# Near scores of the second prompt half: 32 consecutive queries against 160 keys, rows put in class order by DMA

## The chip, the core and the metric

The kernel runs on one core of one Trainium2 chip. The metric is device time in microseconds (us) of one execution; lower is better. The core has TensorE (PE, with its weight loads PEld), VectorE (DVE), ScalarE (ACT), GpSimd (POOL) and SyncE (SP), which only issues DMAs here. SBUF has 128 partitions; matmuls accumulate in PSUM.

## The reference, cut to what matters

One layer of a decoder for a prompt of 256 tokens and 32 sample tokens, all in f32. One input projection gives, among others, q, k and v for three groups of four heads of dimension 128. Group g attends to keys at distances that are multiples of its dilation (1, 4, 16):

```
GROUPS = ((128, 1), (512, 4), (2048, 16))          # window, dilation
valid = (du >= 0) & (du <= BAND) & (uk >= 0)       # BAND = 128 steps of the dilation
sc = q . k * ATT_SCALE - slope * distance, -inf where not valid
p = softmax(sc); o = p @ v
# head j of the three groups is merged with weights softmax(lse) over the groups
```

So a token of group 0 (dilation 1, "near") can see itself and the 128 tokens before it: 129 keys. Merging three groups by their log-sum-exp equals one softmax over the keys of all three groups, and the kernel computes it so. Around the attention stand a gated convolution, two large projections, two layer norms and a feed-forward part of width 5632.

## The kernel before, in words

All activations lie with features on partitions and the 288 tokens on the free axis. Nearly all time goes into `product` (L237): one block of 128 output features, 16 blocks of 128 inputs, three matmuls each (high and low part of the weights and of x in a 32-bit replicated form), so 48 matmuls of 288 columns. The weights of a block come as a 1 MB DMA into `wst` (three buffers, `prepare`, L194), then ACT casts the high part (`whi`) and DVE subtracts it to get the low part (`wlo`), in two halves (`split`, L263). There are four half buffers, so the split of a block starts when PE is done with a half of the block two before it.

The order of the work on each engine is settled when the program is built: the framework simulates a timeline and places each instruction by priority of program order and by when it expects it to be ready. `behind(i, after)` adds an order edge without a wait. `prepare`, called in `product`, traces a block's load and split ahead of the matmuls of the block before; after each `product`, `prompt_step` (L228) pops some queued small copies (`soon`) and runs the next step of the current prompt generator, up to its next `yield`.

The prompt attention works in four classes c: token t belongs to class t mod 4 (NC = 4, NW = 32 tokens per class and half). For groups 1 and 2 a query needs keys of its own class only. So queries, scores and weights of a half h (128 tokens) are stored in class order: partition c*32+i holds token 4*i+c. The scores of a half are one row of SBUF, `s_half[h]`: first the near columns (128 for h = 0, 256 for h = 1), then the far columns of groups 1 and 2.

`score_row(heads)` (L471) issues the score matmuls on PE in a fixed row: for each head, half, group and class one matmul with 32 stationary columns (the queries of that class) that writes 32 partitions of PSUM (L490). For the near group all four quadrants take the same keys: the first 128 for h = 0, all 256 for h = 1, though a query of the second half can see only 129 of them; the rest is masked by large distances in `m_near[1]`. If weights of earlier heads are waiting (`o_next`), `output_row` (L430, matmuls at L443) follows at once in the same row.

`softmax(j, s3)` (L506) adds the distance penalties on DVE (L512), one instruction per half and group, from PSUM into `s_half`; then for each half reduce_max (L519), scaling by -SCALE (L520), exp with a sum on ACT (L521), reciprocal and scaling (L522, L523). `weights(p)` then transposes all scores in blocks of 32 (L455, one DVE instruction) into `s_squares`, and `moved` copies the blocks to their places: the diagonal ones on POOL (L459), the others on ACT (L463) or DVE (L461) from the queue `soon`. `no_keys` (L504) is a memset on POOL that masks the far columns without keys in the first half.

`three_heads` (heads 2, 0, 1 in this order; two steps each) and `last_head` (head 3) are the generators that run these; `last_head` begins with the score row that also holds the outputs of the first three. Beside them `sample_steps` runs the sample's attention on POOL, ACT and DVE over 1 MB cache tiles. `load_distances(h)` (L396) brings the distances into SBUF, rows in class order: `m_near[h]` and, through `m_all[h]`, `m_far` (L406). At L843 the queries are copied from PSUM into `q_all` in class order (L846).

Of the kernel before, what the change touches and what calls it, by code (L numbers as in the profile page):

```python
# [12 lines left out]
AF = mybir.ActivationFunctionType  # L13
ALU = mybir.AluOpType
AX = mybir.AxisListType
PSUM = bass.MemoryType.PSUM

P = 128
D = 2048
KD = D // P  # L20
SEQ = 256
# [13 lines left out]
NG, NH = 3, 4  # L35
DIL = (1, 4, 16)
BAND = 128
SCALE = P**-0.5
# [4 lines left out]
BIG = 1e30  # L43
# [4 lines left out]
NC = 4  # L48
NI = SEQ // NC
NW = P // NC  # L50

NQ = P // 32
N_NEW = NT + NG - 1
MB = 1 + 2 + 2
SLOPE = [[float(np.float32(2.0 ** (-8.0 * (g * NH + j + 1) / (NG * NH)))) for j in range(NH)] for g in range(NG)]
# [52 lines left out]
def layer_kernel(ctx: ExitStack, tc: tile.TileContext, ins, outs):  # L108
# [14 lines left out]
    def sb(pl, shape, tag, dt=F32, bufs=None):  # L123
        return pl.tile(shape, dt, tag=tag, name=nm(tag), bufs=bufs)
# [22 lines left out]
    w_load = [None]  # L147
# [3 lines left out]
    def behind(i, after):  # L151

        tc.add_manual_dep(i.ins, after.ins.name, no_sync, reason="pace")
# [202 lines left out]
    def pa_take(n):  # L356
        pa_at[0] += n
        return pa[:, pa_at[0] - n : pa_at[0]]


    m_near = [pa_take((1 + h) * P) for h in range(2)]
    m_all = [pa_take((NG - 1) * (1 + h) * P).rearrange("p (g k) -> p g k", g=NG - 1) for h in range(2)]
    k_third = [m_all[1].rearrange("p g k -> p (g k)")[:, g * SEQ : (g + 1) * SEQ] for g in range(NG - 1)]
    k_first = pa_take(SEQ)
    m_far = pa_take(2 * (NG - 1) * NI).rearrange("p (h g k) -> p h g k", h=2, g=NG - 1)

# [29 lines left out]
    def load_distances(h):  # L396

        c0, nk = (C_M0, C_M1)[h], (1 + h) * P
        m = ins["cst"][:, c0 : c0 + NG * nk].rearrange("(i c) (g k) -> c i g k", c=NC, g=NG)
        for c in range(NC):  # L400
            at = slice(c * NW, (c + 1) * NW)
            behind(sp.dma_start(m_near[h][at], m[c, :, 0]), w_load[0])
            behind(sp.dma_start(m_all[h][at], m[c, :, 1:]), w_load[0])
        for c in range(NC):
            at = slice(c * NW, (c + 1) * NW)
            pool.tensor_copy(  # L406
                m_far[at, h, :, : (1 + h) * NW], m_all[h][at].rearrange("p g (i c) -> p c g i", c=NC)[:, c]
            )

    def in_a_row(row):  # L410

# [13 lines left out]
    def far_keys(h, g):  # L425

        at = (1 + h) * P + (g - 1) * NI
        return slice(at, at + (1 + h) * NW)
# [42 lines left out]
    def score_row(heads):  # L471

        s3 = []
        w = P + (NG - 1) * NW
        first = att()
        row = [last_mm[0]]
        for n, (j, kT, k_class) in enumerate(heads):
            second = sb(ps, [P, 512], *(("att", F32, 2), ("long", F32, 1), ("acc",))[n])
            near_at = second[:, 3 * P :] if n == 2 else first[:, n * w : n * w + P]
            far_at = first[:, n * w : (n + 1) * w - P] if n == 2 else first[:, n * w + P : (n + 1) * w]  # L480
            s3.append([
                [near_at, *(far_at[:, g * NW : (g + 1) * NW] for g in range(NG - 1))],
                [second[:, far_keys(1, g) if g else slice(0, 2 * P)] for g in range(NG)],
            ])
            for h in range(2):
                for g in range(NG):
                    for c in range(NC):
                        at = slice(c * NW, (c + 1) * NW)
                        k = k_class[g - 1][:, c, : (1 + h) * NW] if g else kT[:, : (1 + h) * P]
                        row.append(pe.matmul(  # L490
                            s3[n][h][g][at], q_all[:, j, g, h * P + c * NW : h * P + (c + 1) * NW], k,
                            start=True, stop=True,
                        ))
        if o_next:
            some_moves(len(soon))
            row += output_row()
        in_a_row(row)
        return s3
# [4 lines left out]
    def no_keys():  # L503
        pool.memset(s_half[0][:, P:].rearrange("p (g k) -> p g k", g=NG - 1)[:, :, NW:], -BIG)  # L504

    def softmax(j, s3):  # L506
        s = s_half
        for h in range(2):
            near = (1 + h) * P
            for g in range(NG):  # L510
                at = far_keys(h, g) if g else slice(0, near)
                dve.scalar_tensor_tensor(  # L512
                    s[h][:, at], m_far[:, h, g - 1, : (1 + h) * NW] if g else m_near[h], -SLOPE[g][j] / SCALE,
                    s3[h][g],
                    ALU.mult, ALU.add,
                )
        for h in range(2):
            st = sb(wk, [P, 4], "st", bufs=4)
            dve.reduce_max(st[:, 0:1], s[h], AX.X)  # L519
            dve.tensor_scalar_mul(st[:, 1:2], st[:, 0:1], -SCALE)  # L520
            act.activation(s[h], s[h], AF.Exp, bias=st[:, 1:2], scale=SCALE, accum_out=st[:, 2:3])  # L521
            dve.reciprocal(st[:, 3:4], st[:, 2:3])  # L522
            dve.tensor_scalar_mul(s[h], s[h], st[:, 3:4])  # L523

    def values(vT):
        squares(v_squares[:, :2], vT[:, 0, :SEQ].rearrange("p (b k) -> p b k", b=2))
# [6 lines left out]
    def weights(p):  # L533

        some_moves(len(soon))
        squares(s_squares, s_all)
        moved(p, s_squares)
# [6 lines left out]
    def three_heads(heads, vT):  # L544

        no_keys()
        s3 = score_row(heads)
        pause[0] = N_PAUSE
        n_moves[0] = N_MOVES_TWO
        for n, j in enumerate((2, 0, 1)):  # L550
            softmax(j, s3[j])
            yield 1
            weights(p_three[j])
            no_keys()
            if n == 0:
                values(vT)
                moved(v_three[2], v_squares, True)
            yield 1
        o_next.extend(zip(range(3), v_three, p_three))

    def last_head(head, vT):

        s3 = score_row([head])
        softmax(head[0], s3[0])
        values(vT)
        moved(late_v, v_squares)
        yield 1
        weights(late_p)
        yield 2
        o_next.append((head[0], late_v, late_p))  # L570
# [272 lines left out]
    for j in range(NH):  # L843
        for g in range(NG):
            q = (q_first.pop(0) if q_first else product(x)).rearrange("p h a -> p (a h)")
            act.copy(  # L846
                q_all[:, j, g].rearrange("p (h c i) -> p h c i", h=2, c=NC),
                q[:, :SEQ].rearrange("p (h i c) -> p h c i", h=2, c=NC),
            )
            act.copy(q_s[:, g, j], q[:, SEQ:])  # L850
            n = j * NG + g
            if n in (5, 7):
                load_distances((n - 5) // 2)
            elif n in (3, 6):
                behind(sp.dma_start(*((cst, ins["cst"][:, :C_BM]) if n == 3 else (prm, ins["prm"]))), w_load[0])
            steps_on[0] = j * NG + g >= NH * NG - 1 - LATER
# [612 lines left out]
```

## Time and profile before

| | |
|---|---|
| median of 3 runs | 1701.44 us (1701.07 to 1701.99) |
| profiled execution | 1701.29 us, of which the span of the trace is 1699.5 us |
| granted clock | 0.999 |
| busy: PE, DVE, ACT, POOL | 100%, 70%, 55%, 23% of the span |
| HBM | 307 GB/s over the span |
| score rows of the prompt | from 182.34 us (heads 0 to 2) and from 220.96 us (head 3 and the outputs of the first three) |

Rows of the profile read: engine, line of the kernel, operation, output and inputs by the program's tile names, shape, count; then busy us and mean ns, and the idle time just before with what ended it. Timeline rows begin with the start in us and the time that the merged row covers. Tile names are those of the memory pools, so several things share one: `yal` holds scores, distances, `by_time` and the high parts of transposed values; `yah` holds queries and weights; `dd` keys and values. SPq and ACTq are the instruction streams that issue DMAs.

### The profile page before, as it was taken

To read this page: it belongs to the slowest core of one execution; us is meant where nothing else is said; L and a number is where in the kernel's file an instruction comes from. 1 tells how busy PE (TensorE), PEld (TensorE's weight loads), DVE (VectorE), ACT (ScalarE), POOL (GpSimd) and SP (SyncE) were. 2 spreads that over 40 slices of the span, in tenths; PEclk is the share of its full clock that TensorE was granted. 3 is DMA by queue.
4 is the path that set the end of the run, shared out by engine and by line. 5 is a ranking of instruction groups with operands and counts; after the bars stand their busy time and mean duration, and the time that the engine had idled before them with its cause. 6 is when DMAs were issued, how large, how long until landed. Compare 5 with 4: busy or idle time off the path is not lost.

```text
span 1699.5 us, 34306 instructions
## 1 busy us (share of the span) xinstructions
PE 1693.1 (100%) x14094; PEld 1689.8 (99%) x14094; DVE 1197.2 (70%) x1549; ACT 941.7 (55%) x1683; POOL 396.7 (23%) x528
## 2 busy tenths in 40 slices
PE   9999999999999999999999999999999999999998
PEld 9999999999999999999999999999999999999998
DVE  5476779889887777655888886776554555555576
ACT  6477686665666655544546664555433454444455
POOL 0122242223332121111454440111100010011175
PEclk9999999999999999999999999999999999999999
DMA  8788778666688889577766668676666666766553
GB/s 316 271 298 351 282 284 314 241 251 245 248 295 311 333 305 337 212 262 255 282 234 225 224 214 322 224 257 226 229 238 225 223 227 248 294 223 250 197 176 113
DMA packets 61532, 436.16 MB, mean 257 GB/s; under 512 B 7936, under 2 KB 11904, under 8 KB 23680
## 3 DMA queue, kind: packets, MB, share of 16 engines
q1 hardware_dynamic: 60080, 430.15, 69.0%
q10 hardware_dynamic: 1296, 3.83, 0.6%
q8 instruction: 110, 1.80, 0.4%
q14 instruction: 46, 0.38, 0.1%
HBM read 427.50 MB, written 94.53 MB: 307 GB/s over the span
## 4 chain that ended last, share of the span: by engine, by line
PE 99%; DMA 0%; DVE 0%; ACT 0%; SPq 0%; issue 0%; ACTq 0%; DVEq 0%
PE acc L257 32%; PE acc L258 32%; PE acc L259 32%; PE acc L342 1%; PE acc L443 0%; DMA yah<-in_x 0%; PE att L490 0%; DVE acc L1140 0%; PE acc L490 0%; SPq L297 0%; DVE yah L1140 0%; ACT xh L309 0%; PE acc L1129 0%; PE acc L1126 0%; PE acc L1125 0%
## 5 line engine op out<-in xcount | busy, mean ns | idle before, releaser
L263 DVE TENSOR_TENSOR wlo<-wst,whi 128x1024 fp32r<-128x1024 f32 (+1 forms) x579 | 744.9, 1288 | 394.0 <-ACT whi L263 391.7
L263 ACT CAST whi<-wst 128x1024 fp32r<-128x1024 f32 (+1 forms) x579 | 588.6, 1019 | 653.8 <-PE acc L258 587.2
L257 PE MATMUL acc<-xh,whi 128*128 128x288 f32 (+1 forms) x3216 | 920.3, 286 | 0.0
L258 PE MATMUL acc<-xl,whi 128*128 128x288 f32 (+1 forms) x3216 | 920.0, 286 | 0.0
L259 PE MATMUL acc<-xh,wlo 128*128 128x288 f32 (+1 forms) x3216 | 920.0, 286 | 0.0
L257 PEld LDWEIGHTS acc<-xh,whi 128*128 128x128 f32 x3216 | 607.8, 189 | 0.5 <-issue 0.4
L258 PEld LDWEIGHTS acc<-xl,whi 128*128 128x128 f32 x3216 | 607.8, 189 | 0.0
L259 PEld LDWEIGHTS acc<-xh,wlo 128*128 128x128 f32 x3216 | 607.8, 189 | 0.0
L258 PE MATMUL acc<-yal,whi 128*128 128x288 f32 x1216 | 347.5, 286 | 0.0
L259 PE MATMUL acc<-yah,wlo 128*128 128x288 f32 x1216 | 347.4, 286 | 0.0
L257 PE MATMUL acc<-yah,whi 128*128 128x288 f32 x1216 | 347.2, 286 | 0.0
L258 PEld LDWEIGHTS acc<-yal,whi 128*128 128x128 f32 x1216 | 229.8, 189 | 0.0
L259 PEld LDWEIGHTS acc<-yah,wlo 128*128 128x128 f32 x1216 | 229.7, 189 | 0.0
L257 PEld LDWEIGHTS acc<-yah,whi 128*128 128x128 f32 x1216 | 229.6, 189 | 0.0
L909 POOL COPY qk_s<-u 128x2 f32<-128x2 f32 x44 | 37.3, 847 | 534.5 <-ACT u L1228 487.0
L897 DVE SCALAR_TENSOR_TENSOR cy<-u,prm,cy 128x304 f32<-128x304 f32 x120 | 70.5, 587 | 7.0 <-ACT cy L895 4.4
L613 POOL TENSOR_TENSOR cache<-cache,cst 128x1024 f32<-128x1024 f32 x16 | 32.8, 2056 | 112.2 <-DMA cache<-in_cv 105.0
L613 POOL TENSOR_TENSOR cache<-cache,qk_s 128x1024 f32<-128x1024 f32 x16 | 32.7, 2045 | 65.6 <-DMA cache<-in_ck 65.3
L920 DVE TENSOR_TENSOR ya<-cy,acc 128x256 f32<-128x256 f32 x104 | 27.6, 308 | 26.7 <-PE acc L259 26.2
L263 ACT CAST yah<-ya 128x288 fp32r<-128x288 f32 x76 | 32.6, 428 | 23.6 <-DVE ya L920 14.6
L611 ACT ACTIVATE cache<-cache,qk_s 128x128 f32<-128x128 f32 x128 | 40.6, 392 | 0.0
L611 ACT ACTIVATE cache<-cache,cst 128x128 f32<-128x128 f32 x128 | 40.0, 389 | 0.0
(282 smaller groups left out, 1186.6 us busy)
## 6 DMA issues: line engine op xcount, KB each, us to landing
wst<-in_w_in SPq DMA_DIRECT2D x112, 1024.0 KB, 5.5
wst<-in_w_up SPq DMA_DIRECT2D x88, 1024.0 KB, 4.9
cache<-in_ck SPq DMA_DIRECT2D x18, 1024.0 KB, 8.3
cache<-in_cv SPq DMA_DIRECT2D x18, 1024.0 KB, 8.5
wst<-in_w_a SPq DMA_DIRECT2D x16, 1024.0 KB, 6.7
wst<-in_w_out SPq DMA_DIRECT2D x16, 1024.0 KB, 4.9
wst<-in_w_down SPq DMA_DIRECT2D x32, 512.0 KB, 4.6
wst<-in_w_down SPq DMA_DIRECT2D x16, 1024.0 KB, 4.9
```

What stands on the lines that cost most here:

```text
L257: pe.matmul(out, hi[:, c, :], xh_k, start=k == 0, stop=False)
L258: pe.matmul(out, hi[:, c, :], xl_k, start=False, stop=False)
L259: last_mm[0] = pe.matmul(out, lo[:, c, :], xh_k, start=False, stop=k == nk - 1)
L263: return act.copy(hi, src), dve.tensor_tensor(lo, src, f32(hi), ALU.subtract)
L342: i = pe.matmul(o[b], first_w(term == 2, b, k), xk, start=k == 0 and term == 0, stop=k == KD - 1 and term == 2,)
L611: behind(act.activation(o[:, a, b], t[:, a, b], AF.Copy, scale=w[:, a, b : b + 1]), w_split[0])
L613: behind(pool.tensor_tensor(o, t, w.unsqueeze(3).broadcast_to([P, *n]), ALU.mult), w_split[1])
L897: dve.scalar_tensor_tensor(y, u[:, i : i + YW], prm[:, w0 + i : w0 + i + 1], y, ALU.mult, ALU.add)
L909: pool.tensor_copy(dst[:, 0:2], u[:, SEQ : SEQ + 2])
L920: dve.tensor_tensor(a, b, c, ALU.mult)
```

## The change

The near scores of the second half are computed for 32 queries in succession in time, t = 32*c to 32*c+31, instead of 32 queries of one class. These need only the 160 keys from 32*c to 32*c+159 (of 256), so each quadrant gets its own window of keys: NB_W = 160. Groups 1 and 2 and the first half stay in class order. The near scores of the second half then come out in time order: DVE adds the penalties per quadrant into the new buffer `by_time` (128 x 256, filled with -BIG once; it lies where the distances `m_all[0]` lay), and four DMAs of SP copy rows c, c+4, c+8, ... of it to quadrant c of `s_half[1]`, after which the softmax goes on as before. `softmax` is divided into `scored` (penalties) and `softmax(h)` (one half), and the order of the steps changes: the penalties of the next head are written in the step of the head before, the DMAs are issued once that head's weights have left `s_half`, and the second half's softmax of the first head comes one step later. The queries of the near group are stored in class order for the first half and in time order for the second, with two copies. The distances `m_near[1]` are loaded as windows of 160.

```diff
+NB_W = P + 32
...
-    m_near = [pa_take((1 + h) * P) for h in range(2)]
+    m_near = [pa_take(n) for n in (P, NB_W)]
+    pa_take(2 * P - NB_W)
...
+    by_time = m_all[0].rearrange("p g k -> p (g k)")
...
-            behind(sp.dma_start(m_near[h][at], m[c, :, 0]), w_load[0])
+            if h:
+                n = c0 + c * NW
+                behind(sp.dma_start(m_near[h][at], ins["cst"][at, n : n + NB_W]), w_load[0])
+            else:
+                behind(sp.dma_start(m_near[h][at], m[c, :, 0]), w_load[0])
...
+        if h:
+            pool.memset(by_time, -BIG)
...
-                [second[:, far_keys(1, g) if g else slice(0, 2 * P)] for g in range(NG)],
+                [second[:, far_keys(1, g) if g else slice(0, NB_W)] for g in range(NG)],
...
-                        k = k_class[g - 1][:, c, : (1 + h) * NW] if g else kT[:, : (1 + h) * P]
+                        if g:
+                            k = k_class[g - 1][:, c, : (1 + h) * NW]
+                        else:
+                            k = kT[:, c * NW : c * NW + NB_W] if h else kT[:, :P]
...
-    def softmax(j, s3):
+    def later_near(j, s3):
+
+        for c in range(NC):
+            at = slice(c * NW, (c + 1) * NW)
+            dve.scalar_tensor_tensor(
+                by_time[at, c * NW : c * NW + NB_W], m_near[1][at], -SLOPE[0][j] / SCALE, s3[1][0][at],
+                ALU.mult, ALU.add,
+            )
+
+    def by_class_rows():
+
+        for c in range(NC):
+            at = slice(c * NW, (c + 1) * NW)
+            behind(sp.dma_start(s_half[1][at, : 2 * P], by_time[c::NC]), w_load[0])
+
+    def scored(j, s3):
         s = s_half
         for h in range(2):
-            near = (1 + h) * P
-            for g in range(NG):
-                at = far_keys(h, g) if g else slice(0, near)
+            for g in range(h, NG):
+                at = far_keys(h, g) if g else slice(0, P)
                 dve.scalar_tensor_tensor(
...
-        for h in range(2):
-            st = sb(wk, [P, 4], "st", bufs=4)
...
+    def softmax(h):
+        s = s_half
+        st = sb(wk, [P, 4], "st", bufs=4)
+        dve.reduce_max(st[:, 0:1], s[h], AX.X)
...
-        for n, j in enumerate((2, 0, 1)):
-            softmax(j, s3[j])
+        order = 2, 0, 1
+        later_near(order[0], s3[order[0]])
+        by_class_rows()
+        for n, j in enumerate(order):
+            scored(j, s3[j])
+            softmax(0)
+            if n:
+                softmax(1)
+            if n < 2:
+                later_near(order[n + 1], s3[order[n + 1]])
             yield 1
+            if n == 0:
+                softmax(1)
             weights(p_three[j])
             no_keys()
+            if n < 2:
+                by_class_rows()
...
     def last_head(head, vT):
 
         s3 = score_row([head])
-        softmax(head[0], s3[0])
+        later_near(head[0], s3[0])
+        by_class_rows()
+        scored(head[0], s3[0])
+        softmax(0)
         values(vT)
         moved(late_v, v_squares)
         yield 1
+        softmax(1)
         weights(late_p)
...
+            n = SEQ if g else P
             act.copy(
-                q_all[:, j, g].rearrange("p (h c i) -> p h c i", h=2, c=NC),
-                q[:, :SEQ].rearrange("p (h i c) -> p h c i", h=2, c=NC),
+                q_all[:, j, g, :n].rearrange("p (h c i) -> p h c i", h=n // P, c=NC),
+                q[:, :n].rearrange("p (h i c) -> p h c i", h=n // P, c=NC),
             )
+            if n < SEQ:
+                act.copy(q_all[:, j, g, n:], q[:, n:SEQ])
```

More of the change, by code (lines that the diff above doesn't have):

```diff
@@ L516, in softmax @@
                 )
-        for h in range(2):
-            st = sb(wk, [P, 4], "st", bufs=4)
[L519 to L523, printed above, removed]
+    def softmax(h):
+        s = s_half
+        st = sb(wk, [P, 4], "st", bufs=4)
+        dve.reduce_max(st[:, 0:1], s[h], AX.X)
+        dve.tensor_scalar_mul(st[:, 1:2], st[:, 0:1], -SCALE)
+        act.activation(s[h], s[h], AF.Exp, bias=st[:, 1:2], scale=SCALE, accum_out=st[:, 2:3])
+        dve.reciprocal(st[:, 3:4], st[:, 2:3])
+        dve.tensor_scalar_mul(s[h], s[h], st[:, 3:4])
     def values(vT):
```

## The prediction

> **What bounds the kernel now.** I read the page first: engines, clock, and the chain that ended last.
>
> ```profile
> span 1699.5 us, 34306 instructions
> PE 1693.1 (100%) x14094; PEld 1689.8 (99%) x14094; DVE 1197.2 (70%) x1549; ACT 941.7 (55%) x1683; POOL 396.7 (23%) x528
> PE 99%; DMA 0%; DVE 0%; ACT 0%; SPq 0%; issue 0%; ACTq 0%; DVEq 0%
> ```
>
> TensorE is busy for 1693.1 of 1699.5 us and it is 99% of the chain (the windows below show its granted clock at 1.00). Then the waits of PE alone, over the whole span:
>
> ```profile
> PE acc L273 <- PEq L1456: 0.8, 1, 0.8
> PE acc L342 <- ACT yal L309: 0.4, 1, 0.4
> ```
>
> These are all its waits, both at the very start. So nothing that another engine does now ends late for PE. Only two things can move the time: PE has less or more to stream, or something becomes so late that PE begins to wait. The change does a little of the first and works on the second.
>
> **PE: what goes.** The timeline of PE over the score rows of the first three heads (start, duration, then the instruction; each group of four quadrants counts 8 because an f32 matmul is recorded as two):
>
> ```profile
> 182.34 0.43 PE L490 MATMUL att<-yal,yah 128*32 128x128 f32 x8
> 182.58 0.31 PE L490 MATMUL att<-u,yah 128*32 128x32 f32 x16
> 182.71 0.62 PE L490 MATMUL att<-yal,yah 128*32 128x256 f32 x8
> 183.14 0.41 PE L490 MATMUL att<-u,yah 128*32 128x64 f32 x16
> 183.36 0.40 PE L490 MATMUL att<-dd,yah 128*32 128x128 f32 x8
> ```
>
> Starts give the throughput. The near group with 256 keys takes 183.14 - 182.71 = 0.43 us, the one with 128 keys 182.58 - 182.34 = 0.24 us. The slope is 0.19 us per 128 keys; 96 keys fewer are worth 0.14 us, or 0.16 us if the whole 0.43 scales with length (0.43 x 96/256). Four heads: 0.57 to 0.64 us. I take 0.6 us. PE has no idle time there, so all of it shortens the span: 0.035%, the entire possible gain on PE.
>
> Each quadrant now gets its own 160 keys instead of one shared stream. Could the four quadrants then run one after the other? The far groups already give each quadrant its own keys, and two groups of 64 keys fit in 0.22 us, which is 0.11 us per group, a quarter of the 0.43 us that 256 keys take. So they overlap. If they did not, four streams of 0.27 us (0.43 x 160/256) would replace 0.43 us: +0.65 us a head, +2.6 us in all.
>
> **Early edits.** Loading the distances has as many DMAs as before (the near one has rows of 160 instead of 256 values), plus one memset of 256 columns on POOL. The query of the near group is copied in two ACT instructions instead of one, four times in the span. The rows around one such copy:
>
> ```profile
> 48.03 0.37 ACT L846 COPY yah<-acc 128x256 f32<-128x256 f32 x1
> 50.02 1.05 ACT L263 CAST whi<-wst 128x1024 fp32r<-128x1024 f32 x1 [1.54 <-PE acc L258]
> ```
>
> ACT sits idle for 1.54 us right behind the copy, waiting for PE. Two copies cost at most twice 0.37 us, so 0.37 us more, inside 1.54 us: nothing. The memset: POOL is 23% busy over the span and nothing on PE waits for it: nothing. Without this cover each copy would delay a cast, four times 0.37 us.
>
> **DVE: what is added.** The score additions, grouped by shape:
>
> ```profile
> L512 DVE SCALAR_TENSOR_TENSOR yal<-yal,att 128x128 f32<-128x128 f32 x3 | 0.8, 278 | 0.0
> L512 DVE SCALAR_TENSOR_TENSOR yal<-yal,att 128x256 f32<-128x256 f32 x2 | 0.8, 409 | 0.0
> L512 DVE SCALAR_TENSOR_TENSOR yal<-yal,att 128x64 f32<-128x64 f32 x4 | 0.7, 211 | 0.0
> ```
>
> One addition of 256 columns (0.41 us) becomes four of 160 columns on 32 partitions. No row has that shape; time goes with columns, so 0.28 us is the lower and 0.41 us the upper bound, 0.31 us by interpolation. Four are 1.24 us (1.12 to 1.64), so +0.83 us a head (+0.71 to +1.23). The stage of the first three heads, from the windows view (busy of PE, PEld, DVE, ACT, POOL, then clock, DMA share, GB/s):
>
> ```profile
> 185.50:197.20 11.70, 11.70 (x99) 11.70 (x96) 8.84 (x30) 7.64 (x18) 4.73 (x9) 1.00 0.59 225
> 197.20:208.90 11.70, 11.70 (x98) 11.70 (x97) 11.04 (x29) 9.66 (x23) 3.38 (x5) 1.00 0.59 216
> 208.90:221.00 12.10, 12.10 (x103) 11.96 (x105) 8.84 (x15) 10.46 (x27) 6.15 (x9) 1.00 0.64 233
> ```
>
> DVE is busy 8.84 + 11.04 + 8.84 = 28.7 of 35.5 us: 6.8 us free, of which 2.5 us are taken. It fits on average, tightest in the middle.
>
> **The new waits.** Each head puts 4 DMAs of 32 KB on SP's queue, from by_time to s_half. Three engines can be held by them. DVE: in the first step it writes the next head's near scores into by_time, after the DMAs have read it; behind that stands the rest (wlo) of a weight split. DVE again: reduce_max of the second half waits for the DMAs to land. SP: the DMAs wait for DVE, and weight loads queue behind them. First SP's loads, the rows being a load, its landing time, and the cast that reads that block three loads later:
>
> ```profile
> 184.65 9.57 SPq L205 DMA_DIRECT2D wst<-in_w_in  x2
> ```
> ```profile
> wst<-in_w_in SPq DMA_DIRECT2D x1, 1024.0 KB, 8.0
> ```
> ```profile
> 200.56 1.05 ACT L263 CAST whi<-wst 128x1024 fp32r<-128x1024 f32 x1
> ```
>
> The load issued at 184.65 lands at 192.65; its cast starts at 200.56. A load may be 7.9 us later at no cost, while the DMAs hold SP only until DVE has written, and then for four issues. Cost: nothing; past 7.9 us SP's delay would reach the cast one for one. Now DVE and the steps that set PE's deadlines:
>
> ```profile
> 185.48 0.39 PE L257 MATMUL acc<-xh,whi 128*128 128x288 f32 x1
> 186.01 0.23 DVE L512 SCALAR_TENSOR_TENSOR yal<-yal,att 128x32 f32<-128x32 f32 x2
> 189.80 0.85 DVE L455 STREAM_TRANSPOSE yah<-yal 128x640 f32<-128x640 f32 x1
> 190.56 1.18 DVE L263 TENSOR_TENSOR wlo<-wst,whi 128x1024 fp32r<-128x1024 f32 x1
> 203.61 0.84 DVE L455 STREAM_TRANSPOSE yah<-yal 128x640 f32<-128x640 f32 x1
> 212.74 0.84 DVE L455 STREAM_TRANSPOSE yah<-yal 128x640 f32<-128x640 f32 x1 [0.20 <-ACT yah L463]
> 220.96 0.42 PE L490 MATMUL att<-dd,yah 128*32 128x128 f32 x8
> ```
>
> From 185.48 to 220.96 PE runs six products, 5.91 us each. The wlo at 190.56 belongs to the third, which starts at 185.48 + 2 x 5.91 = 197.3. It ends at 191.74 now, so DVE has 5.6 us to give.
>
> How long do the DMAs take? The nearest rows are other DMAs of 16 to 64 KB, loaded early between weight loads: 32 KB ones, then the issue times in ns and the spread of landing of one line's.
>
> ```profile
> yal<-in_cst SPq DMA_DIRECT2D x8, 32.0 KB, 5.5
> ```
> ```profile
> L403 SPq DMA_DIRECT2D yal<-in_cst x8: 311/417/443, 25.6 to 40.9; - x8
> ...
> DMA to landing us min/median/max: 1.8/5.5/7.6
> ```
>
> So an issue takes 0.42 us, and L, from issue to landing, lies between 1.8 and 7.6 us. For the first head I take 5.3 us: near scores ready at 186.0 + 1.24 = 187.2, last issue 3 x 0.42 = 1.3 us later, and the load of 184.65 lands at 192.65, with the class rows behind it. For the other two the DMA share is about 0.6: 0.6 x 5.5 + 0.4 x 1.8 = 4.0 us, my choice. The first wait on DVE then ends at 187.2 + 1.3 + 5.3 = 193.8; adding 1.24 us and wlo's 1.18 us, wlo ends at 196.2 even if it is queued behind: 1.1 us before its deadline. Hidden, but not by much; past L = 6.4 us it would cost PE one for one, at this place.
>
> The weights' chain is the second deadline. Where PE reads them (moves of the second head's weights on ACT, then the output row on PE):
>
> ```profile
> 216.18 0.66 ACT L463 COPY yah<-yah 32x160 f32<-32x160 f32 x2
> 217.56 2.00 ACT L463 COPY yah<-yah 32x160 f32<-32x160 f32 x6
> 219.57 1.32 ACT L463 COPY yah<-yah 32x160 f32<-32x160 f32 x4
> 221.98 2.38 PE L443 MATMUL acc<-yah,yal 128*32 128x256 f32 x96
> 224.17 1.28 PE L443 MATMUL acc<-yah 128*32 128x256 f32 x48
> 225.38 0.39 PE L257 MATMUL acc<-xh,whi 128*128 128x288 f32 x1
> ```
>
> The last head in order is the second of three in the row, so PE needs it about a third into 221.98 to 225.38: 223.1. Its 12 moves take 3.98 us, so the transpose ahead of them (212.74 to 213.58 now) must end by 219.1. The chain after the change, with half a softmax at 2.3 us:
>
> ```profile
> 186.96 0.86 DVE L519 TENSOR_REDUCE st<-yal 128x1 f32<-128x256 f32 x2
> 189.34 0.42 DVE L523 TENSOR_SCALAR yal<-yal,st 128x384 f32<-128x384 f32 x1
> ```
>
> (From 187.4, the middle of the two reductions, to 189.76 where the last scaling ends.) First transpose done at 187.2 + 1.3 + L + 1.24 + 2.3 + 0.85 = 192.9 + L. Each further head: 1.3 + L + 2.3 + 0.85 and one wlo of 1.2 us, 5.7 + L. The third ends at 204.3 + the three landings: 204.3 + 5.3 + 4.0 + 4.0 = 217.6, against 219.1. Later than now by 4 us, and still 1.5 us early. Cost on PE: nothing, while L is at most 4.9 us on average.
>
> The Trainium skill (DMA: Bandwidth & Descriptors, Queues, rings and completion order) speaks against this: each DMA engine takes the descriptors of one queue in ring order, so that a small DMA stands behind any load on SP's queue. If a load stood ahead each time, L would be the 5.5 us of the rows above, and the sum 1702.4 us (worked out as a rival below). The same page (Anatomy of one DMA) gives about 2.0 us fixed plus bytes over 436 GB/s, an estimate of 2.1 us for 32 KB; by that alone the sum stays at 1700.7 us. Of the two the median agrees with the first, the shortest row (1.8 us) with the second.
>
> The fourth head's output is far behind (its other steps lie in a stage with more slack); its chain costs nothing.
>
> **Sum.** PE -0.6 us, all else 0. The profiled execution took 1701.29 us (span 1699.5 and 1.8 around it); that gives 1700.7 us. The median of the runs is 0.15 us above it, so 1700.8 us is my forecast. About 0.2%, 3.4 us, is what a measurement of this kernel can tell from no change: I forecast no difference that can be told.
>
> **Rivals.** *The weights come late for the output row (slower).* Mechanism: three landings in series, place: before the second part of the row at 223.1. At the median of 5.5 us the last transpose ends at 204.3 + 16.5 = 220.8, PE idles 1.7 us, and the time is 1702.4 us. For a loss over 3.4 us PE must idle 4.0 us, which needs L = 6.3 us on average; at the longest, 7.6 us, it ends at 227.1, 8.0 us late: 1708.7 us. For: 5.5 us is the median of the only rows of that size, and the middle window is 94% busy on DVE. Against: those rows were queued 16 at a time between loads, and here the DMA share is 0.6. I give 0.27 to a small idle (0.3 to 4 us) and 0.14 to a large one.
>
> PE's first matmuls of the span last 449 ns each:
>
> ```profile
> L273 PE MATMUL acc<-const-float32-0.0 128*128 128x288 f32 x16 | 4.1, 449 | 0.8 <-PEq L1456 0.8
> ```
>
> The Trainium skill (TensorE: Matmul & The Clock Gate, Part 1) says that an idle window of about 3.4 us halves the clock until PE has been busy as long again. So the large idle has a further price: about 3.4 us at half rate, an estimate by that page, 1.7 us more. The row above shows slow matmuls at the start, after an idle PE; no row here shows it in the middle of the span.
>
> *The quadrants run in succession.* +2.6 us, 1703.9 us, still within 0.2%. Against it stand the far groups. Chance 0.03.
>
> *The order changes elsewhere.* Sixteen more DMAs and 12 more additions could let the program's planner place something better; the gain would have to come out of PE's 1.2 us of waits and cannot reach 3.4 us by any row here. Chance of faster 0.01.
>
> **How the numbers follow.** No idle: 0.55; small idle 0.27, large 0.14, quadrants 0.03, faster 0.01. Within 0.2%: 0.55 + 0.27 + 0.03 = 0.85. The range starts at 1699.9 us (0.64 us gained and 0.4 us of spread below the median of the runs) and reaches to 1704.5 us, an idle of 3.7 us, which takes in the quadrants' case and nearly all of the small idles, about 0.8.
>
> **What would show it.** Near groups with 160 keys that take 0.27 to 0.29 us from start to start; PE with no new wait; DVE waits of a few us behind the new DMAs; L near 4 to 5 us; the last transpose of the three near 217. A PE wait in the output row, or on wlo near 197, shows the rival; near groups of 0.4 us or more show the quadrants. A time over 1704.9 us would make the forecast wrong.

## The result, and the profile after

The changed kernel takes 1707.7 us (median of 6 runs, 1707.12 to 1708.11) against 1701.34 us for the kernel before: ratio 1.0037, 95% interval 1.0024 to 1.005. It is slower by 6.4 us, where no difference was forecast; the time lies outside the range, near the slower rival's 1708.7 us. The profiled execution took 1707.55 us, with a span of 1705.8 us. (Line numbers move by up to 47; what was L443, L455, L463, L490 and L512 is L452, L464, L472, L502 and L522 or L538.)

TensorE gained what was forecast. In the timeline of PE after, the near group of 160 keys takes 183.07 - 182.80 = 0.27 us instead of 0.43:

```profile
182.80 0.46 PE L502 MATMUL att<-yal,yah 128*32 128x160 f32 x8
183.07 0.41 PE L502 MATMUL att<-u,yah 128*32 128x64 f32 x16
```

The whole score row of three heads runs from 182.44 to 185.09 us: 2.65 us instead of 3.14. The quadrants overlap. But PE now waits. Its waits over the whole span, those of the start left out (us in total, times, longest):

```profile
PE acc L452 <- ACT yah L472: 2.8, 1, 2.8
...
PE acc L260 <- DVE wlo L264: 0.7, 2, 0.5
...
PE acc L260 <- issue: 0.2, 1, 0.2
```

The wait of 2.8 us is in the output row, for ACT's moves of weights. The rows of PE there, and the two groups of moves that it waits for:

```profile
222.84 1.28 PE L452 MATMUL acc<-yah,yal 128*32 128x256 f32 x48
226.94 2.36 PE L452 MATMUL acc<-yah,yal 128*32 128x256 f32 x48 [2.82 <-ACT yah L472]
229.04 1.76 PE L452 MATMUL acc<-yah 128*32 128x256 f32 x48
230.73 0.39 PE L258 MATMUL acc<-xh,whi 128*128 128x288 f32 x1
```
```profile
222.80 1.66 ACT L472 COPY yah<-yah 32x160 f32<-32x160 f32 x5 [0.59 <-DVE yah L464]
224.47 2.32 ACT L472 COPY yah<-yah 32x160 f32<-32x160 f32 x7
```

The moves end at 226.79 and PE goes on at 226.94. Before, the three heads' outputs took 3.40 us, starts at equal distances; now 230.73 - 222.84 = 7.89 us. The second head's 48 matmuls alone take 2.10 us, about twice their 1.1. The windows view says why (the last columns are granted clock, DMA share and GB/s):

```profile
222.80:224.10 1.30, 1.30 (x65) 0.88 (x53) 1.30 (x2) 1.26 (x4) 1.23 (x2) 1.00 0.06 25
224.10:226.90 2.80, 0.02 (x4) 0.00 (x0) 1.77 (x3) 2.68 (x10) 2.02 (x7) 0.94 0.74 143
226.90:229.00 2.10, 2.06 (x48) 1.70 (x52) 1.10 (x1) 2.10 (x3) 0.00 (x0) 0.50 1.76 732
```

The granted clock fell to 0.50 at the end of the idle stretch. It is 0.50 from 226.6 to 230.0 us, 3.4 us in all. So the 4.49 us lost in this row are 2.8 us of idling and 1.7 us that are, but for about 0.2 us, the lower clock: the two heads' 96 matmuls take 2.10 + 1.69 = 3.79 us instead of 2.27.

ACT's moves are late because the scores are transposed late. DVE's transposes of the three heads (189.80, 203.61 and 212.74 us before) and the wait ahead of the first:

```profile
193.42 1.31 DVE L522 SCALAR_TENSOR_TENSOR yal<-yal,att 32x160 f32<-32x160 f32 x4 [1.97 <-DMA yal<-yal]
...
197.20 0.85 DVE L464 STREAM_TRANSPOSE yah<-yal 128x640 f32<-128x640 f32 x1
...
211.94 0.84 DVE L464 STREAM_TRANSPOSE yah<-yal 128x640 f32<-128x640 f32 x1
...
221.92 0.85 DVE L464 STREAM_TRANSPOSE yah<-yal 128x640 f32<-128x640 f32 x1
```

The first is 7.4 us late, the second 8.3, the third 9.2. From one to the next it takes 14.7 and 10.0 us, against 13.8 and 9.1 before. The account of the span, from starts of the same row in both traces: 0.10 us late at the first score row, -0.49 us in it, +1.12 us up to the second score row, where PE stops for late splits (the rows show 0.17 and 0.51 us of idling), +0.13 in its scores, +4.49 us in the output row, +0.45 us up to the last head's output (384.3 and 390.1), 0.0 from there to the last normalisation, and about 0.5 us behind PE's last product, which no experiment followed: +6.3 us.

### The profile page after: what moved, and what is told of

It is laid out like the page before. It is cut to its first block, busy times and chain, and to the rows that moved or that the text cites. A ratio compares the mean times of both kernels' runs of the same rounds, so it can differ in the third digit from the quotient of the medians.

```text
span 1705.8 us, 34355 instructions
## 1 busy us (share of the span) xinstructions
PE 1695.0 (99%) x14094; PEld 1691.0 (99%) x14094; DVE 1203.6 (71%) x1561; ACT 941.9 (55%) x1687; POOL 397.4 (23%) x529
## 4 chain that ended last, share of the span: by engine, by line
PE 84%; DVE 0%; ACT 0%; issue 0%; ACTq 0%; DVEq 0%
PE acc L260 28%; PE acc L258 28%; PE acc L259 28%; DVE acc L1187 0%; DVE wlo L264 0%; PE acc L452 0%; ACT whi L264 0%; DVE yah L1187 0%; PE acc L1176 0%; PE acc L1172 0%; PE acc L1173 0%; PE att L1091 0%; ACT yah L1197 0%; ACTq L1511 0%; DVE yah L1192 0%
## 5 line engine op out<-in xcount | busy, mean ns | idle before, releaser
L657 POOL TENSOR_TENSOR cache<-cache,qk_s 128x1024 f32<-128x1024 f32 x16 | 33.4, 2087 | 63.9 <-ACT whi L264 30.3
```

The costliest lines, as they stand in the source:

```text
L657: behind(pool.tensor_tensor(o, t, w.unsqueeze(3).broadcast_to([P, *n]), ALU.mult), w_split[1])
```

## The experiments

Each is compared with the kernel before on the same chip (medians of 1701.37 to 1701.47 us there). The changed kernel's 1707.7 us is the other mark. My theory after the result: the DMAs' issue and landing make the first head's weights late, and everything after inherits it. The rival: the new order and the added DVE work do it, with the DMAs hidden.

**No DMAs.** In `by_class_rows` the four DMAs go; the columns that they fill are set once.

```diff
     def by_class_rows():
-        for c in range(NC):
-            at = slice(c * NW, (c + 1) * NW)
-            behind(sp.dma_start(s_half[1][at, : 2 * P], by_time[c::NC]), w_load[0])
+        pass
```

> The kernel after without the DMAs of class rows: by_time is written but never copied, and the near columns of the second half hold a constant set once, so the near scores of the second half do not enter the result. All else, the divided softmax and its order of steps too, stays. Landing theory (the weights are late because each head waits for its DMAs to be issued and to land): the first transpose of scores ends near 192 us instead of 198.1, the third before 219.1 instead of 222.8, PE has no wait in the output row, the clock stays at 1.00 there, and the time is 1700.7 to 1701.5 us. Order theory (the weights are late because of the divided softmax, the added instructions and where they stand in DVE's queue, and the DMAs are hidden): the third transpose still ends after 221, PE idles 1.5 us or more, and the time stays above 1704 us.

1700.46 us, ratio 0.9994 (0.9985 to 1.0003). PE has no wait but those at the start of the span. The transposes:

```profile
194.07 0.84 DVE L465 STREAM_TRANSPOSE yah<-yal 128x640 f32<-128x640 f32 x1
...
206.74 0.85 DVE L465 STREAM_TRANSPOSE yah<-yal 128x640 f32<-128x640 f32 x1
...
215.97 0.84 DVE L465 STREAM_TRANSPOSE yah<-yal 128x640 f32<-128x640 f32 x1
```

The third ends at 216.8, before the limit of 219.1 us. So the divided softmax, its order and the added instructions cost no time by themselves; the loss of 7.2 us comes with the DMAs. They do use up slack: the first transpose ends at 194.9, not near 192 as the landing theory had it, because the additions of the next two heads now stand ahead of it on DVE. The time without DMAs is 1.0 us below the kernel before, not to be told from none.

**DMAs that nobody waits for.** The same DMAs write to unused columns.

```diff
-            behind(sp.dma_start(s_half[1][at, : 2 * P], by_time[c::NC]), w_load[0])
+            behind(sp.dma_start(xs_flat[at, NH * NG * SEQ + 2 * MB * P :], by_time[c::NC]), w_load[0])
```

> The kernel after with all its DMAs of class rows, but into unused columns of SBUF, so that no softmax waits for them; the near columns of the second half hold a constant set once, so the near scores of the second half do not enter the result. If waiting for the landing is the cost: transposes within 2 us of those without DMAs (194.9, 207.6 and 216.8), no wait in the output row, 1700.3 to 1702 us. If it is the DMAs' own load (SP's queue held, weight loads late, bytes on the DMA engines): the time stays above 1704 us and PE waits on casts or splits.

1701.23 us, ratio 1.0001 (0.9992 to 1.001). The transposes:

```profile
191.42 0.84 DVE L465 STREAM_TRANSPOSE yah<-yal 128x640 f32<-128x640 f32 x1
...
205.97 0.84 DVE L465 STREAM_TRANSPOSE yah<-yal 128x640 f32<-128x640 f32 x1
...
215.09 0.84 DVE L465 STREAM_TRANSPOSE yah<-yal 128x640 f32<-128x640 f32 x1 [0.20 <-ACT yah L473]
```

SP's time, the bytes and the later weight loads make PE wait for nothing; what costs is that the softmax waits for the landing. (One wait for the DMAs is still there, 0.80 us of DVE until they have read `by_time`.) The 0.8 us over the kernel without DMAs lie behind PE's last product: from there to the end of the span it is 5.8 us before, 6.2 after the change, 6.2 here and 5.4 without DMAs. The cause of that stays open.

This run also divides the lateness. Counted from each run's own score row, the third transpose starts after 30.4 us before, 39.5 us after the change, 32.1 us here and 33.4 us without DMAs. Of the 9.1 us, then, 1.7 to 3.0 us are the new order and the added instructions, which the slack of 5.5 us holds, and the rest comes with the wait for the DMAs.

**Only the first head without DMAs.**

```diff
         later_near(order[0], s3[order[0]])
-        by_class_rows()
```

> The kernel after without the DMAs of the first of the three heads alone; the other heads keep theirs. That head's near scores of the second half are a constant, so they do not enter the result. If the first head's wait makes the loss (its transpose is 7.4 us late, the other two add 0.9 us each): the first transpose is back near 192 to 194.5, the third ends by 218, no wait in the output row, and the time is 1700.5 to 1702 us. If each head's landing adds a third: the third transpose ends at 220 or later and the time is 1703.5 us or more.

1703.22 us, ratio 1.0012 (1.0003 to 1.0021): above the first theory's 1702 and below the rival's 1703.5. The transposes are back:

```profile
192.76 0.84 DVE L465 STREAM_TRANSPOSE yah<-yal 128x640 f32<-128x640 f32 x1
...
207.37 0.84 DVE L465 STREAM_TRANSPOSE yah<-yal 128x640 f32<-128x640 f32 x1
...
216.60 0.85 DVE L465 STREAM_TRANSPOSE yah<-yal 128x640 f32<-128x640 f32 x1
```

The wait in the output row is gone, and the time is 4.5 us below that after the change. (The other two heads' DMAs land after 1.8 us in this run, so it does not show what their longer landings would cost without the first wait.) 2.8 us above the kernel without DMAs remain. About 0.8 us of them lie behind PE's last product, as above; the larger part is PE waiting near 250 us for the cast and the split of one block, the first two of these rows:

```profile
PE acc L260 <- DVE wlo L264: 0.7, 1, 0.7
PE acc L258 <- ACT whi L264: 0.6, 1, 0.6
PE acc L260 <- issue: 0.3, 1, 0.3
```

There the last head's DMAs hold DVE: a split waits 0.78 us for them and reduce_max 0.74 us.

**Weight loads behind the DMAs.** An order edge puts, for each head, the load of 1 MB that stood ahead of its DMAs on SP behind them.

```diff
+        if n in hold:
+            behind(d, hold[n])
...
-            behind(sp.dma_start(s_half[1][at, : 2 * P], by_time[c::NC]), w_load[0])
+            hold[loads[0] + 4] = sp.dma_start(s_half[1][at, : 2 * P], by_time[c::NC])
+            behind(hold[loads[0] + 4], w_load[0])
```

> The kernel after with three weight loads of 1 MB put behind a head's DMAs of class rows on SP's queue (an order edge, no other change); each of them is read some 8 us after it lands now, so the delay should cost nothing by itself. If the small DMAs land late because a load is moving at the same time: landing falls from 4.5 to 5.7 us to 2 to 3.5 us for the first two heads, the third transpose ends 3 us earlier or more (219.8 or before), and the time falls by 2 us or more to below 1705.7. If the landing time is the small DMAs' own (issue, 32 KB rows, completion): it stays near 5 us, the time stays within 1 us of 1707.7 or rises by late loads.

1705.67 us, ratio 1.0025 (1.0016 to 1.0035). Landing times of the three heads' DMAs, first after the change, then here:

```profile
yal<-yal SPq DMA_DIRECT2D x4, 32.0 KB, 4.5
...
yal<-yal SPq DMA_DIRECT2D x4, 32.0 KB, 5.7
...
yal<-yal SPq DMA_DIRECT2D x4, 32.0 KB, 3.3
```
```profile
yal<-yal SPq DMA_DIRECT2D x4, 32.0 KB, 2.5
...
yal<-yal SPq DMA_DIRECT2D x4, 32.0 KB, 1.8
...
yal<-yal SPq DMA_DIRECT2D x4, 32.0 KB, 1.8
```

So the small DMAs land late because a load is under way. But the transposes hardly follow:

```profile
196.28 0.85 DVE L467 STREAM_TRANSPOSE yah<-yal 128x640 f32<-128x640 f32 x1
...
210.89 0.84 DVE L467 STREAM_TRANSPOSE yah<-yal 128x640 f32<-128x640 f32 x1
...
220.87 0.85 DVE L467 STREAM_TRANSPOSE yah<-yal 128x640 f32<-128x640 f32 x1
```

The third ends at 221.7, where 219.8 or less was expected. From one to the next it still takes 14.6 and 10.0 us with landings of 1.8 us, and 14.6 and 9.1 us where no softmax waits for a DMA. So the landing does not set the first of these steps, and at most 0.9 us of the second. DVE's queue does, with its waits for ACT's casts. After the change it reads, between the first and the second transpose:

```profile
198.74 1.22 DVE L264 TENSOR_TENSOR wlo<-wst,whi 128x1024 fp32r<-128x1024 f32 x1
...
202.18 1.22 DVE L264 TENSOR_TENSOR wlo<-wst,whi 128x1024 fp32r<-128x1024 f32 x1 [1.01 <-ACT whi L264]
...
203.90 2.90 DVE L470 COPY yah<-yal 32x192 f32<-32x192 f32 x11
...
206.91 0.53 DVE L547 TENSOR_REDUCE st<-yal 128x1 f32<-128x384 f32 x1
207.36 1.30 DVE L522 SCALAR_TENSOR_TENSOR yal<-yal,long 32x160 f32<-32x160 f32 x4
208.69 1.23 DVE L264 TENSOR_TENSOR wlo<-wst,whi 128x1024 fp32r<-128x1024 f32 x1
...
210.16 1.22 DVE L264 TENSOR_TENSOR wlo<-wst,whi 128x1024 fp32r<-128x1024 f32 x1
```

Four splits of weights (4.9 us) and twelve copies of values (3.15 us, one of them ahead of the row shown) stand in this step; most of the copies, two splits and the next head's additions lie between the parts of one softmax. Among the three heads only the first shows a wait of DVE for the DMAs, here 1.14 us instead of 1.97, and nothing behind it gives time back. The 2.0 us that this version wins (1.5 us between the two profiled executions) are mostly late splits, which PE no longer waits for; the idle of 2.8 us in the output row is still there.

**Two buffers for the scores in time order**, so that DVE need not wait until the DMAs have read.

```diff
+    times = [(by_time, xs_flat[:, NH * NG * SEQ + 2 * MB * P :])[b] for b in (1, 0, 0, 1)]
...
-                by_time[at, c * NW : c * NW + NB_W], m_near[1][at], -SLOPE[0][j] / SCALE, s3[1][0][at],
+                times[j][at, c * NW : c * NW + NB_W], m_near[1][at], -SLOPE[0][j] / SCALE, s3[1][0][at],
```

> The kernel after with two buffers for the near scores in time order, in turn, so that DVE can write the next head's scores without waiting until the DMAs have read the last one's. The DMAs themselves and the wait for their landing stay. If the write-after-read wait of DVE (2.0 us before the first head's second softmax) is what matters: the first transpose ends near 196.7 instead of 198.05, the third near 220 or earlier, and the time falls by 2 us or more to below 1705.7. If the wait for the landing matters (reduce_max of the same half waits for the same DMAs): the first transpose ends at most 1.3 us earlier, the third within 1.5 us of 222.8, and the time stays at 1706 to 1707.7 us.

1705.91 us, ratio 1.0027 (1.0017 to 1.0037). The first transpose starts at 197.32, no earlier, the third at 220.47: DVE now waits for the landing in reduce_max instead. The time lies between the two expectations, and the reason is another: PE idles 2.44 us in the output row instead of 2.82, and its clock does not fall, as the windows behind the idle show:

```profile
225.40:228.00 2.60, 2.51 (x97) 2.11 (x98) 1.55 (x3) 2.60 (x5) 1.27 (x4) 1.00 1.69 707
```

**Both edits together**, two buffers and the loads behind:

```diff
+            hold[loads[0] + 4] = sp.dma_start(s_half[1][at, : 2 * P], times[j][c::NC])
+            behind(hold[loads[0] + 4], w_load[0])
```

> Two buffers and the loads put behind together. If both waits are links of one chain, the gains add: the third transpose ends before 219 us, PE has no wait in the output row, and the time is 1701 to 1703 us. If the delay has another cause, the time is that of the better of the two alone.

1704.19 us, ratio 1.0016 (1.0007 to 1.0025). The gains add. The two steps between the transposes take 13.3 and 8.3 us here instead of 14.7 and 10.0, so some of the delay can be made up. But the third still ends at 220.1 and PE idles 1.6 us: better than either, worse than hoped, and still slower than before.

**Both, with the next head's additions traced behind the transpose.**

```diff
-            if n < 2:
-                later_near(order[n + 1], s3[order[n + 1]])
             yield 1
...
             weights(p_three[j])
+            if n < 2:
+                later_near(order[n + 1], s3[order[n + 1]])
```

> Two buffers and loads put behind (as in e8_both), and the next head's near scores are added on DVE after the head's scores have been transposed, instead of in front of its second half's softmax. If DVE's queue between the landing and the transpose is what is left of the delay (in e8_both the additions, 1.3 us, stand between reduce_max and the scaling): each of the first two transposes ends about 1.3 us earlier, the third before 219 us, PE idles less than 0.5 us in the output row, and the time is 1701 to 1702.5 us. Rival (the DMAs then start later by the same amount, so nothing is won): the third transpose stays near 220 and the time at 1704.2 us.

1703.84 us, ratio 1.0015 (1.0006 to 1.0024), not to be told from the version above. The planner placed the additions where they were, as soon as the scores were there, so this decides nothing:

```profile
192.77 0.55 DVE L553 TENSOR_REDUCE st<-yal 128x1 f32<-128x384 f32 x1 [0.42 <-DMA yal<-yal]
193.24 1.30 DVE L527 SCALAR_TENSOR_TENSOR yal<-yal,long 32x160 f32<-32x160 f32 x4
```

**Half of the DMAs from POOL.**

```diff
-            hold[loads[0] + 4] = sp.dma_start(s_half[1][at, : 2 * P], times[j][c::NC])
+            d = (sp, pool)[c % 2].dma_start(s_half[1][at, : 2 * P], times[j][c::NC])
```

> As e9_near_after, with two of each head's four DMAs issued from POOL's queue instead of SP's. SP takes 2.4 us to issue four; if this issue time is a link of the chain, the first transpose ends 1 us earlier than in e9_near_after and the time falls by up to 1 us, not below 1700.7. Rival (POOL's issue is slower, or its copies of weights are held up by it): the transposes come later, the time rises by 1 us or more.

1717.23 us, ratio 1.0093 (1.0078 to 1.0107): the rival. POOL issues behind its own copies of weights, and the second head's two land after 7.7 us while SP's take 1.8; the third transpose starts at 231.63 and PE idles 13.9 us:

```profile
yal<-yah SPq DMA_DIRECT2D x2, 32.0 KB, 1.8
yal<-yah POOLq DMA_DIRECT2D x2, 32.0 KB, 7.7
```

**All DMAs from ACT's queue.**

```diff
-            behind(sp.dma_start(s_half[1][at, : 2 * P], by_time[c::NC]), w_load[0])
+            behind(act.dma_start(s_half[1][at, : 2 * P], by_time[c::NC]), w_split[0])
```

> The kernel after with the DMAs of class rows issued from ACT's queue instead of SP's, so that they do not stand behind the 1 MB weight loads in one queue; ACT has to wait for DVE and to issue (4 x 0.57 us a head at SP's rate). Ring-order theory (small DMAs wait for the load ahead of them in their queue): landing falls from 5.2 us (median) to 3 us or less, the first transpose comes 1.5 us or more earlier, and the time falls by 1 to 4 us, unless ACT's casts become late. Shared-engines theory (all queues run on the same DMA engines, and the load takes its time from any queue): landing stays at 4.5 us or more, and the time stays within 1.5 us of 1707.7 or rises, since ACT is held.

1725.15 us, ratio 1.014 (1.0126 to 1.0154). Off the loads' queue the DMAs land after 4.4 us in the median, instead of 5.2, just under the 4.5 us of the second theory; for the first three heads it is 4.6, 6.6 and 4.1 us, no shorter than the 4.5, 5.7 and 3.3 us on SP. So sharing a queue with the load is not what slows them. What is left is that they share the DMA engines with it. ACT meanwhile is held by the waits ahead of its DMAs, and PE waits for its moves:

```profile
PE acc L452 <- ACT yah L472: 15.7, 1, 15.7
```

The Trainium skill (DMA: Bandwidth & Descriptors, Issuing engines are not separate DMA queues) says that DMAs of all issuing engines run on the same 16 DMA engines and interleave. The landings above agree.

**PE kept busy in the idle stretch.**

```diff
         for n_o, (j, v, p) in enumerate(o_next):
             po = sb(ps, [P, SEQ], "acc")
+            if n_o == 1:
+                row += [pe.matmul(po, zeros[0], zeros[1][:, :SEQ], start=True, stop=True) for _ in range(24)]
```

> The kernel after with 24 matmuls on zeros (256 columns, 0.11 us each, 2.6 us in all) put between the first and the second head of the output row, where PE now idles 2.8 us. They compute nothing that is used. Clock theory (the 96 matmuls after the idle are slow because the granted clock fell to 0.50 in the idle): the remaining idle is below 0.5 us, the clock stays at 1.00, the 48 matmuls of the second head take 1.1 us instead of 2.1, the time falls by about 1.7 us to 1706.0 us. Rival (they are slow because each waits for another piece of the weights): the second head's matmuls take 2 us again and the time stays at 1707.7 us.

1708.46 us, ratio 1.0043 (1.003 to 1.0055). The second head's matmuls now run from 227.56 to 228.68, 1.12 us, at a clock of 1.00:

```profile
227.56 1.30 PE L454 MATMUL acc<-yah,yal 128*32 128x256 f32 x48
228.68 1.28 PE L454 MATMUL acc<-yah 128*32 128x256 f32 x48
```

That confirms the clock as the cause of the slow rows. But the time did not fall to 1706.0 us as expected; it rose by 0.8 us. PE, 1.4 us earlier (counted from the first score row), met the next late split.

```profile
244.09 0.39 PE L260 MATMUL acc<-xh,wlo 128*128 128x288 f32 x1 [1.76 <-DVE wlo L264]
```

**The outputs one product later.**

```diff
-        if o_next:
-            some_moves(len(soon))
-            row += output_row()
         in_a_row(row)
         return s3
...
         yield 1
+        some_moves(len(soon))
+        in_a_row([last_mm[0]] + output_row())
         softmax(1)
         weights(late_p)
```

> The kernel after with the outputs of the first three heads one product (5.9 us) later on PE, instead of in the score row of the last head; everything else the same. Deadline theory (the loss is paid in the output row, where PE stands idle until ACT has moved the second head's weights, and then runs at half clock): the idle of 2.8 us and the slow matmuls behind it (1.7 us) go, the granted clock is 1.00 throughout, and the time falls by about 4.5 us to 1703.2 us, less if the late splits and moves behind it have slack too. Rival (DVE and ACT are behind by so much that the same delay shows up at the next split of weights): PE waits on wlo or whi for 2 us or more instead, and the time stays above 1706 us.

1707.44 us, ratio 1.0036 (1.0022 to 1.005). The idle in the output row is gone, its clock is full, and the time is the same: the rival. PE stops five times instead, 4.1 us in all: four times for a cast or a split, and once, 0.96 us in the product behind the moved outputs, for nothing that the profile shows. Those after 245 us are

```profile
249.78 0.39 PE L260 MATMUL acc<-xh,wlo 128*128 128x288 f32 x1 [0.75 <-DVE wlo L264]
253.37 0.39 PE L258 MATMUL acc<-xh,whi 128*128 128x288 f32 x1 [0.64 <-ACT whi L264]
254.71 0.39 PE L260 MATMUL acc<-xh,wlo 128*128 128x288 f32 x1 [0.83 <-DVE wlo L264]
```

**The same, without the last head's DMAs.** Its four DMAs, issued from 233 us on, land after 6.2 us.

```diff
         later_near(head[0], s3[0])
-        by_class_rows()
```

> As e2_output_later (outputs one product later), and without the DMAs of the last of the four heads; its near scores of the second half are then those left by the head before, so its result is not the layer's. In e2_output_later PE waits for late weight splits between 235 and 255 us (five waits, 4.1 us with the one at 235). If the last head's wait for its DMAs holds DVE and ACT there: the waits after 245 us go, 2 us or more, and the time falls to 1705.4 us or less. If it is the first three heads' late work that is being made up: the waits on splits stay at 3 us or more in all and the time stays above 1706.5 us.

1704.85 us, ratio 1.0021 (1.0012 to 1.003), 2.6 us less. The last head's transpose starts at 238.92 instead of 243.54, and of the waits after 245 us one of 0.35 us is left. So the last head's DMAs hold up the queues there, and that is where much of the saved idle was spent again. That it is the wait for them and not their load is taken from the version whose DMAs nobody waits for; no run shows it for this order.

## Why the prediction was wrong

- *PE gives 0.6 us, the quadrants overlap*: right. 0.49 us in the first score row, and 0.6 us from the first score row to PE's last product in the two versions where PE waits for nothing (no DMAs, and DMAs that nobody waits for).
- *ACT's extra copies, the memset, SP's longer queue and DVE's additions cost nothing*: right for the time. All of these are in the kernel whose DMAs nobody waits for, at 1701.23 us. But the new order and the additions take 1.7 to 3.0 us of the 5.5 us of slack. Four additions take 1.30 us, 1.24 was forecast.
- *Landings of 5.3, 4.0 and 4.0 us*: right in sum, 4.5 + 5.7 + 3.3 = 13.5 us against 13.3, which is luck, since each is off by 0.7 to 1.7 us. Order in one queue does not explain them, as the DMAs from ACT's queue show. The estimate of 2.1 us from the Trainium skill (DMA: Bandwidth & Descriptors, Anatomy of one DMA) uses a fit that the page gives for DMAs issued from GpSimd; SP's took 1.8 us where no load moved.
- *First transpose done at 198.2*: 198.05. Four issues took 2.46 us in place of the 1.7 reckoned.
- **The step that failed: "Each further head: 1.3 + L + 2.3 + 0.85 and one wlo of 1.2 us, 5.7 + L."** This gave 9.7 us a head and 217.6 us for the third transpose; they took 14.7 and 10.0 us, and it ended at 222.77. So 5.0 of the 5.2 us by which the end was missed are the second head's step. I built each step from its own chain, with one split of 1.2 us and no copies, as if DVE had nothing else; in that step DVE did four splits, 4.9 us, and twelve copies of values, 3.15 us. The rows that I quoted, 189.80 and 203.61, show 13.8 us for it without any DMA, and with landings of 1.8 us (loads behind) it still takes 14.6. The third head's 10.0 us are near the 9.7 by luck: DVE does not wait for its DMAs at all. The first head's delay of 7.4 us, part of it the new order, is therefore handed on whole: 213.58 + 7.4 = 221.0 would have been past 219.1 without a formula.
- *The limit of 219.1 us for the third transpose*: right. The transpose ended 3.7 us past it; PE idled 2.8 us, since the row began 0.86 us later too.
- *A large idle lowers the clock*: named as a further price of the rival, by the Trainium skill (TensorE: Matmul & The Clock Gate, Part 1), and it came, about 1.5 us, after 2.8 us of idling, less than the 3.4 us that the page names.
- *The fourth head costs nothing*: wrong, and put at nothing without a row. Without the DMAs of the first head alone PE waits 1.4 us behind the last head's, and with the outputs moved later the last head's DMAs are worth 2.6 us.
- *The range starts at 1699.9 us*: its two terms, 0.64 and 0.4 us below the median of 1701.44, give 1700.4. Nothing hangs on it here.

The forecast's likeliest case fell. Its slower rival, given 0.14 for a large idle, is right in the place: the weights come late for the output row. It is not right in the cause, which is a first delay handed on by DVE's queue and not three long landings, and that its 1708.7 us is near is luck: it stands for landings of 7.6 us and an idle of 8.0 us, where 4.5 us in the mean and 2.8 us were measured, with the clock and late splits on top. Not settled are the time behind PE's last product and how the rest of the loss divides over the second and third head: experiments that take one wait away let another appear.

## What to carry to other kernels

Before putting a DMA into a chain of small steps, look for the place where PE will need the chain's end, and count how late the end is now: the slack there (here 5.5 us for the third transpose) is all there is, and a chain on a busy engine catches up little, since its pace is set by the queue and not by its own links alone. Here two buffers and the loads behind took back 3 of the 9 us. Take the pace from the rows of the trace, from one head's step to the next, rather than from a sum of durations. A fill of PE's idle time, or a later deadline, gains nothing while the engines that feed PE are behind; the gain of the edit (0.6 us) was too small to pay for the waits it brought.

## What the runs showed of the hardware

The granted clock fell to 0.50 for 3.4 us with idles of 2.82 and 2.81 us, and stayed at 1.00 with idles of 2.44 and 1.58 us. The length of one idle does not decide it, however. After the change the clock fell 0.4 us before PE went on, and with the loads behind 0.9 us after it. With the DMAs on ACT's queue it fell at 210.7 us, within the second of two idles of 2.06 and 1.47 us; PE had been busy for 0.56 us from 207.0 to 210.6 us. So these runs give no threshold.

A DMA of 32 KB within SBUF landed in 1.8 us where no load moved (second and third head, loads behind) and in 3.3 to 5.7 us beside a weight load of 1 MB on SP's queue, 4.1 to 6.6 us from ACT's (first three heads). An issue of such a DMA held SP for 0.57 us in the median, where those of the distances took 0.42.
